# Last gate and final norm with half of the tokens on the partitions

## The chip, the cores and the metric

The kernel runs on one core of one Trainium2 chip. The metric is the device time of one execution in microseconds (us), as the median of several runs. Before the change it is 1174.45 us (median of 3 runs, 1174.26 to 1174.66).

## The reference

A decoder trunk of two layers over 512 tokens of 1024 features, in float32. Layer 0 is a gMLP mixer, layer 1 a sliding-window attention; after each mixer come a gated MLP (`conv_ffn`) and a gated per-layer embedding, and a final norm closes it. The change touches the last two steps for layer 1:

```python
def rmsnorm(x, g):
    xf = x.astype(jnp.float32)
    y = xf * lax.rsqrt(jnp.mean(xf * xf, axis=-1, keepdims=True) + EPS)
    return (y * g.astype(jnp.float32)).astype(x.dtype)

def per_layer_embed(h, p_i, g_norm, w_in, w_gate, b_gate):
    gate = jax.nn.sigmoid(rmsnorm(h, g_norm) @ w_gate + b_gate)
    return (p_i @ w_in) * gate

    h = h + conv_ffn(rmsnorm(h, norm_ffn[i]), f_w_up[i], f_conv_w[i], f_conv_b[i], f_w_down[i])
    h = h + per_layer_embed(h, p[i], norm_ple[i], ple_w_in[i], ple_w_gate[i], ple_b_gate[i])
return rmsnorm(h, norm_final)
```

In the kernel `p_i @ w_in` is called pin, `rmsnorm(h, g_norm) @ w_gate` gate.

## The kernel before, in words

**Layout.** The residual h lies feature-major: eight tiles `h[m]` of 128 features (on the partitions) by 512 tokens. A dense product is computed for one row block of 128 output features at a time: the weights are the stationary operand, the tokens the moving one.

**Precision.** Each float32 operand is split in two float32r halves, hi and lo. A product is three passes on TensorE (PE): hi x hi, lo x hi, hi x lo (`mm3`, lines 168 to 170; `mm3t`, lines 179 to 181, has the tokens as the stationary operand and so gives tokens on the partitions).

**Weight stream.** A list of pieces (`plan`, `plan_cols`, `plan_ffn`) is written ahead in the order of use. `load` (L124) brings a piece from DRAM with one DMA on SP's queue into one of three raw buffers (r0 to r2); `pump` splits it, hi on ScalarE (ACT, L141), lo on VectorE (DVE, L142), into a ring of `WBUFS` buffers (wh, wl) or, for the last two gate pieces, into tiles of their own (own_ah, own_al), which take the places of activations of the FFN that are no longer read. `chunk` hands the split pieces to the products. A load waits until its raw buffer's last split is done.

**Order of work.** PE's instructions stand in the order in which the program writes them, as do those of each other engine except where a scheduler moves an instruction ahead of others by priority. `ffn(1)` computes the up products in three parts; before the last part's down products stands `ple_in(1)` (pin: 48 matmuls of 512 columns, copied out of PSUM by ACT, L360). Then `dense_add` gives d0 to d7 (21 matmuls each), added to h by DVE (L301). As each h[m] is done, `Norm.take` scales and splits it into np1h and np1l (L210 on ACT, L211 on DVE), ACT squares it (L239) and POOL adds the squares up (L244).

**The tail (lines 704 to 799).** The gate is computed in two halves of the tokens, 256 moving columns each, in blocks of two row blocks (`gate(hf, c)`): 24 matmuls for a row block, k from 0 to 7 with three passes each. After gate(0, 0) `npl.begin` takes the mean square (`np1ms`, L255: four small products, then np1m on DVE and the inverse root np1rt on POOL, L268 and L270); after gate(0, 1) `npl.rstd` brings it onto the free dimension: np1dh and np1dl on DVE (L280, L281: a diagonal of the roots), np1sp on PE (L284, ones x diagonal), np1rstd on ACT (L262). `gated` is for each row block: z = gate x rstd (DVE, L725), sigmoid with the bias on its partitions (ACT, L727), times pin (DVE, L728), added to h (DVE, L730), squared (ACT, L732), the squares summed up on POOL (L739). `final_root(0)` stands behind the second half's first gate block, `final(0)` (spread, then y = h x gain x root on DVE, L759, with output DMAs of 256 KB) behind its second. For the second half the residual is turned token-major at the end: `dgain` (L751, diagonal matrices of the final gain, made early on DVE), `turn_back` (L783: 16 plain float32 products h x dgain, six row blocks ahead of the last root and two behind it), `final_root(1)` (L746), and y = ht x root on ACT (L798) and DVE (L796), out by four DMAs of 256 KB on ACT's and SP's queues (L799).

**At the start**, POOL makes small constants (ident, far, qscale), then waits for wsT's DMA (L433) and later computes n0rt (L270), while SP's queue loads vec, h and the first pieces of w_v, and PE begins the v products.

Of the kernel before, what the change touches and what calls it, by code (L numbers as in the profile page):

```python
# [8 lines left out]
F32 = mybir.dt.float32  # L9
# [4 lines left out]
P = 128  # L14
# [7 lines left out]
SLOTS = 9  # L22
HEADS = 16
# [23 lines left out]
def tile_yoco(ctx: ExitStack, tc: tile.TileContext, t, out: bass.AP, out_b: bass.AP):  # L47
# [26 lines left out]

    def plan_cols(w, n_chunks, kk, cols=256, k0=0):
        for c in range(n_chunks):
            plan(w[c, :, k0 * cols : (k0 + kk) * cols], kk * cols, cols)

# [38 lines left out]
    def load(upto):  # L117
        while state["raw"] < min(upto, len(pieces)):
# [5 lines left out]
            nc.sync.dma_start(r[:, :m], a)  # L124
# [27 lines left out]
    def chunk(cols, kk, ahead=WBUFS):  # L152
        """The next units that make up kk row blocks of `cols` columns, a triple for each."""
# [8 lines left out]
    def mm3(ps, parts, xs, c0, n=P, first=True, last=True):  # L162
        """ps += W[:, c0:c0+n]^T x over the row blocks, as three float32r passes."""
# [8 lines left out]
    def mm3t(ps, xs, parts, c0, n, tok, first=True, last=True):  # L172
        """ps += x[tokens]^T W[:, c0:c0+n]: tokens on partitions."""
# [9 lines left out]
    # ---- activations in  # L183
# [24 lines left out]
    # ---- helpers on activations  # L208
# [16 lines left out]
    class Norm:  # L225
        """Takes the residual's row blocks as they come: gains and splits them, sums the squares."""
# [24 lines left out]
        def begin(self):  # L251
            """One over the root mean square, tokens on the partitions."""
# [6 lines left out]
        def rstd(self):  # L259
            """The same along the free dimension, for every partition."""  # L260
# [12 lines left out]
    def spread(r, n, name):  # L273
        """[P, n] with tokens on the partitions -> [P, n * P], the tokens along it, in PSUM."""
# [18 lines left out]
    def dense_add(xs, kk, norm):  # L293
        """h += W^T x for the next kk row blocks of weights, 256 columns a chunk."""
# [10 lines left out]
    def ffn(l, norm, nxt):  # L305
        """Gated MLP, the hidden units in parts; the first of the next part goes before a part's products down."""
# [42 lines left out]
    def ple_in(l):  # L349
# [12 lines left out]
        return pe  # L362

# [22 lines left out]
    # ---- layer 0: gMLP mixer  # L386
# [26 lines left out]
    # minus the distance to the key, far away where the window or causality forbids it  # L413
# [7 lines left out]
    # queries over eight times a head's slope: logit = slope * (q k - distance)  # L421
# [10 lines left out]
    # positions attend to earlier ones alone: wsT[s, h, t] for s <= t  # L432
# [49 lines left out]

    npl = Norm("np0", [(xp, "x", gain("norm_ple", 0))])
# [4 lines left out]
    # ---- layer 1: shared K/V and sliding-window attention  # L488
# [3 lines left out]
    # keys of a group, their halves twice on the partitions, for the stacked halves of the queries  # L492
# [51 lines left out]
    # products beside attention's steps: each step is followed by some that need no result of it  # L544
# [21 lines left out]
    def merge(m, k0, k1):  # L566
        """Row block m of the output projection, from the heads that are done."""
# [36 lines left out]
    def scores(i):  # L604
        """Logits of a group's four heads over a block, their maximum with the sink, the exponentials."""
# [28 lines left out]
    def weights(i):  # L634
        """The exponentials over their sums."""
# [11 lines left out]
    def turn(i):  # L647
        """Probabilities, keys on the partitions."""
# [59 lines left out]
    N = S // 2  # L708
    half = [slice(hf * N, (hf + 1) * N) for hf in range(2)]
    parts, acc, last_sq, root = [], {}, {}, {}  # L710

    def gate(hf, c):
        if hf == 0:
            parts.append(chunk(256, KD))
        pss = []
        for j in range(2):
            ps = psum(f"gate{hf}_{c}_{j}")[:, :N]
            mm3(ps, parts[c], [(a[:, half[hf]], b[:, half[hf]]) for a, b in xs], j * P)
            pss.append(ps)
        return pss  # L720

    def gated(hf, c, pss):
        for m, ps in zip((2 * c, 2 * c + 1), pss):
            z = tp.tile([P, N], F32, tag="hs", name=f"z{hf}_{m}")
            nc.vector.tensor_mul(z, ps, rstd[:, half[hf]])  # L725
            sg = tp.tile([P, N], F32, tag="sg", name=f"gs{hf}_{m}")
            nc.scalar.activation(sg, z, AF.Sigmoid, bias=v("ple_b_gate", KD + m))  # L727
            nc.vector.tensor_mul(sg, sg, pe[m][:, half[hf]])  # L728
            hm = h[m][:, half[hf]]
            nc.vector.tensor_add(hm, hm, sg)  # L730
            sq = tp.tile([P, N], F32, tag="sq", name=f"fsq{hf}_{m}")
            nc.scalar.activation(sq, hm, AF.Square)  # L732
            if m == KD - 1:
                last_sq[hf] = sq
            elif m == 0:
                acc[hf] = sq
            else:
                a = tp.tile([P, N], F32, tag="c0", name=f"facc{hf}_{m}")
                nc.gpsimd.tensor_add(a, acc[hf], sq)  # L739
                acc[hf] = a  # L740

    def final_root(hf):
        ps = psum(f"fms{hf}")
        for c in range(N // P):
            for i, a in enumerate((acc[hf], last_sq[hf])):
                nc.tensor.matmul(ps[:, c : c + 1], a[:, c * P : (c + 1) * P], mean, start=i == 0, stop=i == 1)  # L746
        root[hf] = inv_root(ps[:, : N // P], f"fin{hf}")

    dgain = mp.tile([P, KD, P], F32, tag="m5", name="dgain")
    for m in range(KD):  # L750
        nc.vector.tensor_scalar_mul(dgain[:, m, :], ident, v("norm_final", m))  # L751

    def final(hf):
        r = spread(root[hf], N // P, f"fin{hf}")
        for c in range(4):
            y = (mp if c == 3 else wp).tile([P, 2, N], F32, tag="m4" if c == 3 else f"r{c}", bufs=1, name=f"y{hf}_{c}")
            for j in range(2):
                m = 2 * c + j
                nc.vector.scalar_tensor_tensor(y[:, j, :], h[m][:, half[hf]], v("norm_final", m), r,  # L759
                                               op0=ALU.mult, op1=ALU.mult)  # L760
            (nc.sync if c % 2 else nc.scalar).dma_start(
                out[2 * c : 2 * c + 2].rearrange("k p s -> p k s"), y)

    held = gate(0, 0)
    npl.begin()
    pss = gate(0, 1)
# [99 lines left out]
```

## Time and profile before

| | |
|---|---|
| median of 3 runs | 1174.45 us |
| span of the profiled execution | 1173.3 us |
| median less span | 1.15 us |
| PE, DVE, ACT, POOL busy | 98%, 65%, 46%, 7% of the span |
| bytes moved | 110.2 MB, 94 GB/s on average |

The span runs from the first to the last event of the profiled execution; the runs' times lie around it by the 1.15 us above. Times in rows of the timeline are microseconds from the span's start: start, duration, engine, line, operation, output<-inputs, how many merged instructions, and in brackets how long the engine had been idle before and what ended that. An engine name with q is its queue's issuing of DMAs. PE's matmuls overlap: a matmul's duration is longer than the distance to the next one, so the pitch (start to start) is what a matmul costs in a row of them. A window row gives the stretch, then busy time and count of PE, PEld, DVE, ACT and POOL, the granted clock, the DMA engines' busy share and GB/s. The groups of instructions give busy time in all and the mean in ns. DMA rows give count, KB and median time from issue to landing.

### The profile page before, as it was taken

Reading aid. Unit: us, or ns where it says so; the run is one execution under the profiler, and the core shown is the slowest. Engines: PE = TensorE matmul, PEld = TensorE weight load, DVE = VectorE, ACT = ScalarE, POOL = GpSimd, SP = SyncE. Lnnn points to the kernel's source line nnn. Section 1 sums busy time; section 2 is a strip of 40 time slices with the busy share of each in tenths; the row PEclk is TensorE's granted clock in tenths of the full one; section 3 lists DMA queues with packets and bytes.
Section 4 is the critical chain, followed back from the end, with each engine's and each line's share of the span. In section 5 each row is a group of like instructions: output and inputs, shape, how many; then the busy total and the mean of one; then the engine's idle time right before and its main releaser. Section 6 shows DMA issues by size and latency. Waiting matters only on the chain.

```text
span 1173.3 us, 14202 instructions
## 1 busy us (share of the span) xinstructions
PE 1152.2 (98%) x5634; PEld 968.3 (83%) x5634; DVE 761.8 (65%) x1229; ACT 543.0 (46%) x919; POOL 80.7 (7%) x86
## 2 busy tenths in 40 slices
PE   7999999999999999999989999999999999999998
PEld 7988888888888888888778767888888888888897
DVE  6365467763676377447779997577635773675665
ACT  5633444431344244445559986444313442345532
POOL 1000210000000000031220001100000000000221
PEclk9999999999999999999989999999999999999999
DMA  8222323322222333232212113322322333223302
GB/s 324 79 108 72 108 72 108 108 74 106 108 72 90 110 104 115 101 111 72 72 37 73 36 37 108 108 97 84 108 107 73 99 99 108 90 94 105 108 1 73
DMA packets 19011, 110.20 MB, mean 94 GB/s; under 512 B 2176, under 2 KB 3584, under 8 KB 8704
## 3 DMA queue, kind: packets, MB, share of 16 engines
q1 hardware_dynamic: 18112, 108.24, 26.5%
q10 hardware_dynamic: 832, 1.05, 0.3%
q8 instruction: 44, 0.72, 0.2%
q14 instruction: 23, 0.19, 0.1%
HBM read 107.19 MB, written 2.10 MB: 93 GB/s over the span
## 4 chain that ended last, share of the span: by engine, by line
PE 90%; DVE 6%; ACT 2%; issue 1%; DMA 0%; SPq 0%; POOLq 0%; POOL 0%; DVEq 0%; ACTq 0%
PE up L168 14%; PE up L170 14%; PE up L169 14%; PE d L168 8%; PE d L170 8%; PE d L169 8%; PE gate L169 2%; PE gate L168 2%; PE gate L170 2%; PE v L179 1%; PE v L180 1%; PE v L181 1%; PE u L168 1%; PE u L170 1%; PE u L169 1%; PE o L168 1%
## 5 line engine op out<-in xcount | busy, mean ns | idle before, releaser
L141 ACT CAST wh<-wraw 128x1024 fp32r<-128x1024 f32 (+1 forms) x198 | 203.0, 1026 | 272.8 <-PE d L169 132.2
L142 DVE TENSOR_TENSOR wl<-wraw,wh 128x1024 fp32r<-128x1024 f32 (+1 forms) x198 | 238.6, 1205 | 134.9 <-ACT wh L141 134.6
L168 PE MATMUL up<-nf00h,wh 128*128 128x512 f32 x352 | 137.2, 390 | 0.0
L168 PE MATMUL up<-nf10h,wh 128*128 128x512 f32 x352 | 137.2, 390 | 0.0
L170 PE MATMUL up<-nf10h,wl 128*128 128x512 f32 x352 | 137.1, 390 | 0.0
L170 PE MATMUL up<-nf00h,wl 128*128 128x512 f32 x352 | 137.1, 389 | 0.0
L169 PE MATMUL up<-nf00l,wh 128*128 128x512 f32 x352 | 137.1, 389 | 0.0
L169 PE MATMUL d<-al,wh 128*128 128x512 f32 x352 | 137.1, 389 | 0.0
L168 PE MATMUL d<-ah,wh 128*128 128x512 f32 x352 | 137.1, 389 | 0.0
L169 PE MATMUL up<-nf10l,wh 128*128 128x512 f32 x352 | 137.1, 389 | 0.0
L170 PE MATMUL d<-ah,wl 128*128 128x512 f32 x352 | 137.1, 389 | 0.0
L325 ACT ACTIVATE c<-hs,vec 128x512 f32<-128x512 f32 x88 | 71.5, 814 | 71.9 <-DVE hs L321 71.1
L326 DVE SCALAR_TENSOR_TENSOR c<-hs,vec,c 128x511 f32<-128x511 f32 x88 | 65.8, 749 | 34.2 <-ACT c L325 34.2
L301 DVE TENSOR_TENSOR h<-h,d 128x512 f32<-128x512 f32 x56 | 38.4, 687 | 73.7 <-PE d L170 73.7
L214 ACT CAST ah<-a 128x512 fp32r<-128x512 f32 x44 | 27.3, 621 | 109.1 <-DVE a L331 109.0
L170 PEld LDWEIGHTS up<-nf10h,wl 128*128 128x128 f32 x352 | 66.1, 188 | 13.8
L170 PEld LDWEIGHTS up<-nf00h,wl 128*128 128x128 f32 x352 | 66.1, 188 | 13.8
L170 PEld LDWEIGHTS d<-ah,wl 128*128 128x128 f32 x352 | 66.1, 188 | 13.7
L169 PEld LDWEIGHTS d<-al,wh 128*128 128x128 f32 x352 | 66.1, 188 | 13.7
L168 PEld LDWEIGHTS up<-nf00h,wh 128*128 128x128 f32 x352 | 66.1, 188 | 13.7
L169 PEld LDWEIGHTS up<-nf10l,wh 128*128 128x128 f32 x352 | 66.1, 188 | 13.6
L168 PEld LDWEIGHTS d<-ah,wh 128*128 128x128 f32 x352 | 66.1, 188 | 13.6
(281 smaller groups left out, 2195.4 us busy)
## 6 DMA issues: line engine op xcount, KB each, us to landing
wraw<-in_w_up SPq DMA_DIRECT2D x44, 1024.0 KB, 4.8
wraw<-in_w_down SPq DMA_DIRECT2D x16, 896.0 KB, 4.6
wraw<-in_w_down SPq DMA_DIRECT2D x8, 1024.0 KB, 4.9
wraw<-in_w_gate SPq DMA_DIRECT2D x8, 1024.0 KB, 4.8
wraw<-in_w_u SPq DMA_DIRECT2D x4, 1024.0 KB, 6.3
wraw<-in_w_out SPq DMA_DIRECT2D x4, 1024.0 KB, 4.7
wraw<-in_w_q SPq DMA_DIRECT2D x4, 1024.0 KB, 4.7
wraw<-in_w_o SPq DMA_DIRECT2D x4, 1024.0 KB, 4.8
```

Of the source, the lines that this page charges most:

```text
L141: nc.scalar.copy(wh[:, :n], src)
L142: nc.vector.tensor_sub(wl[:, :n], src, wh[:, :n].bitcast(F32))
L168: nc.tensor.matmul(ps, wh[:, a:b], xh, start=st, stop=False)
L169: nc.tensor.matmul(ps, wh[:, a:b], xl, start=False, stop=False)
L170: nc.tensor.matmul(ps, wl[:, a:b], xh, start=False, stop=en)
L179: nc.tensor.matmul(ps, xh[:, s], wh[:, a:b], start=st, stop=False)
L180: nc.tensor.matmul(ps, xl[:, s], wh[:, a:b], start=False, stop=False)
L181: nc.tensor.matmul(ps, xh[:, s], wl[:, a:b], start=False, stop=en)
L214: nc.scalar.copy(hi, src)
L301: nc.vector.tensor_add(h[m], h[m], ps)
L325: nc.scalar.activation(c, hs, AF.Identity, bias=v("conv_b", l * 2 * NJ + col), scale=cw[2])
L326: nc.vector.scalar_tensor_tensor(c[:, 1:], hs[:, : S - 1], cw[1], c[:, 1:], op0=ALU.mult, op1=ALU.add)
```

## The change

The gate and the final norm are computed feature-major for the first 256 tokens alone. For the second 256 tokens they are computed token-major.

- Pin: `ple_in_both` gives pef (feature-major, first half: 8 row blocks x 6 matmuls of 256 columns) and pet (token-major, second half: 2 token blocks x 2 x 6 matmuls of 512 columns).
- Gate weights of layer 1: `plan_pair` puts two column chunks side by side, four row blocks deep, in one piece; `load` brings it with two DMAs of 512 KB.
- First half: four row blocks open together in PSUM, first with k 0 to 5 for all, then k 6 and 7; `npl.begin` after the first of the four is complete, `npl.rstd` after all four.
- Then the second half's residual is transposed (16 products with ident, copied out by ACT to hT), and row blocks 4 to 7 of the first half follow.
- Second half: token blocks in cuts of 512 and 512 columns, the last in 512, 384 and 128. `gated_t`: z = gate x rt + bias row (DVE), sigmoid (ACT), times pet, plus hT (DVE), square with accumulation (ACT), times the gain row (POOL, the last cut on DVE); `final_t`: sum, inverse root, y scaled on ACT and DVE, two DMAs of 256 KB.
- The bias and the gain as rows: two DMAs on POOL's queue bring 1024 numbers each from the transposed view of vec into DRAM (`lines`), and two DMAs on SP's queue later broadcast them over the partitions (brow, grow).
- `dgain` and `turn_back` are gone. The first half's y is one tile, with four DMAs.

In the changed program's own order the two line DMAs stand among POOL's first instructions (one ahead of the last affine select of far, one behind it), and the row broadcasts on SP's queue ahead of the gate's loads. All other instructions up to pin stand as before. Lines after 706 of the kernel before are replaced as a whole; the diff shows the new ones alone there.

```diff
 SLOTS = 9
+N = S // 2
 HEADS = 16
...
             plan(w[c, :, k0 * cols : (k0 + kk) * cols], kk * cols, cols)
+    def plan_pair(w, k0, k1, own=None):
+        a_ = w[:, :, k0 * 256 : k1 * 256].rearrange("c p (k n) -> p k c n", n=256)
+        plan(a_, (k1 - k0) * S, S, own)
     def plan_ffn(l):
...
     plan_ffn(1)
-    plan_cols(t["w_gate"][1], 2, KD)
     free = [j % SLOTS for j in range(NJ, NJ + 8)]
     for c in range(2):
-        plan(t["w_gate"][1, 2 + c], 2 * UNIT, 256,
-             own=[(ap, f"ah{q}", f"al{q}") for q in free[4 * c : 4 * c + 4]])
+        for k0 in (0, 4):
+            plan_pair(t["w_gate"][1, 2 * c : 2 * c + 2], k0, k0 + 4,
+                      [(ap, f"ah{q}", f"al{q}") for q in free[k0 : k0 + 4]] if c else None)
     units = [(i, q, lo, n) for i, p in enumerate(pieces) for q, (lo, n) in enumerate(p[2])]
...
             state["turn"] += 1
-            nc.sync.dma_start(r[:, :m], a)
+            if len(a.shape) == 4:
+                for c in range(2):
+                    nc.sync.dma_start(r[:, :m].rearrange("p (k c n) -> p k c n", c=2, n=256)[:, :, c], a[:, :, c])
+            else:
+                nc.sync.dma_start(r[:, :m], a)
             raws[j] = r
...
             if last:
-                pe = ple_in(l)
+                pe = ple_in_both() if l else ple_in(l)
             nact = [] if last else [up(j1)]
...
         return pe
+    def ple_in_both():
+        pw = chunk(S, 2)
+        px = [(a[:, o : o + S], b[:, o : o + S]) for a, b, o in pw]
+        first = [(a[:, :N], b[:, :N]) for a, b in px]
+        feat, tok = [], []
+        for c in range(2):
+            parts = chunk(256, 4)
+            pf = mp.tile([P, 4, N], F32, tag=f"m{c}", name=f"pef{c}")
+            for j in range(4):
+                ps = psum(f"pinf{c}_{j}")[:, :N]
+                mm3(ps, parts[j // 2 * 2 : j // 2 * 2 + 2], first, j % 2 * P)
+                nc.scalar.copy(pf[:, j, :], ps)
+                feat.append(pf[:, j, :])
+            wh, wl = (x.rearrange("p (q k n) -> p q k n", q=2, k=2) for x in parts[0][:2])
+            for i in range(2):
+                if c == 0:
+                    tok.append(mp.tile([P, D], F32, tag=f"m{2 + i}", name=f"pet{i}"))
+                ps = psum(f"pint{c}_{i}")
+                s = slice(N + i * P, N + (i + 1) * P)
+                for k, (xh, xl) in enumerate(px):
+                    nc.tensor.matmul(ps, xh[:, s], wh[:, :, k, :], start=k == 0, stop=False)
+                    nc.tensor.matmul(ps, xl[:, s], wh[:, :, k, :], start=False, stop=False)
+                    nc.tensor.matmul(ps, xh[:, s], wl[:, :, k, :], start=False, stop=k == 1)
+                nc.scalar.copy(tok[i][:, c * S : (c + 1) * S], ps)
+        return feat, tok
     def ple(l, norm, nxt, pe):
...
     dense_add(us, KD, nf)
+    dram = ctx.enter_context(tc.tile_pool(name="dram", bufs=1, space=bass.MemoryType.DRAM))
+    lines = []
+    for name, l in (("ple_b_gate", 1), ("norm_final", 0)):
+        c0 = VEC[name] + l * KD
+        line = dram.tile([KD, P], F32, name=f"line_{name}")
+        with nc.allow_non_contiguous_dma(reason="1024 numbers"):
+            nc.gpsimd.dma_start(line, t["vec"][:, c0 : c0 + KD].rearrange("p m -> m p"))
+        lines.append(line.rearrange("m p -> (m p)"))
     npl = Norm("np0", [(xp, "x", gain("norm_ple", 0))])
...
     npl = Norm("np1", [(xp, "x", gain("norm_ple", 1))])
-    pe = ffn(1, nf, npl)
...
+    pef, pet = ffn(1, nf, npl)
+    xs = npl.xs[0][0]
+    half = slice(0, N)
+    first = [(a[:, half], b[:, half]) for a, b in xs]
+    facc = {}
+    def gated(m, ps):
+        z = tp.tile([P, N], F32, tag="hs", name=f"z{m}")
+        nc.vector.tensor_mul(z, ps, rstd[:, half])
+        sg = tp.tile([P, N], F32, tag="sg", name=f"gs{m}")
+        nc.scalar.activation(sg, z, AF.Sigmoid, bias=v("ple_b_gate", KD + m))
+        nc.vector.tensor_mul(sg, sg, pef[m])
+        hm = h[m][:, half]
+        nc.vector.tensor_add(hm, hm, sg)
+        sq = tp.tile([P, N], F32, tag="sq", name=f"fsq{m}")
+        nc.scalar.activation(sq, hm, AF.Square)
+        if m == 0:
+            facc[0] = sq
+        else:
+            a = tp.tile([P, N], F32, tag="c0", name=f"facc{m}")
+            nc.gpsimd.tensor_add(a, facc[0], sq)
+            facc[0] = a
+    parts = chunk(S, KD)
+    pss = [psum(f"gate{m}")[:, :N] for m in range(4)]
+    for m in range(4):
+        mm3(pss[m], parts[:6], first[:6], m * P, last=False)
+    for m in range(4):
+        mm3(pss[m], parts[6:], first[6:], m * P, first=False)
+        if m == 0:
+            rt = npl.begin()
+    rstd = npl.rstd()
+    for m in range(4):
+        gated(m, pss[m])
+    hT = [[at.tile([P, S], F32, tag=f"a{x}{i}", name=f"hT{i}_{x}") for x in "hl"] for i in range(2)]
+    for i in range(2):
+        for q in range(2):
+            ps = psum(f"ht{i}_{q}")
+            for m in range(4):
+                nc.tensor.transpose(ps[:, m * P : (m + 1) * P], h[4 * q + m][:, N + i * P : N + (i + 1) * P], ident)
+            nc.scalar.copy(hT[i][q], ps)
+    parts2 = chunk(S, KD, ahead=2 * WBUFS)
+    for m in range(4):
+        ps = psum(f"gate{4 + m}")[:, :N]
+        mm3(ps, parts2, first, m * P)
+        gated(4 + m, ps)
+    brow, grow = (mp.tile([P, D], F32, tag=tag, name=f"row_{tag}") for tag in ("m4", "m5"))
+    for r, line in zip((brow, grow), lines):
+        nc.sync.dma_start(r, line.partition_broadcast(P))
+    ssq = const.tile([P, 2, 4], F32, name="ssq")
+    total = const.tile([P, 2], F32, name="total")
+    rfin = const.tile([P, 2], F32, name="rfin")
+    yt = [wp.tile([P, D], F32, tag=f"r{1 + i}", bufs=1, name=f"yt{i}") for i in range(2)]
+    cuts = [[(0, 512), (512, 512)], [(0, 512), (512, 384), (896, 128)]]
+    def gate_t(i, n):
+        c0, w = cuts[i][n]
+        ps = psum(f"gt{i}_{n}")[:, :w]
+        mm3t(ps, xs, parts2 if c0 >= S else parts, c0 % S, w, 2 + i)
+        return ps
+    def gated_t(i, n, ps):
+        c0, w = cuts[i][n]
+        end = i == 1 and n == len(cuts[i]) - 1
+        z = tp.tile([P, w], F32, tag="hs", name=f"zt{i}_{n}")
+        nc.vector.scalar_tensor_tensor(z, ps, rt[:, 2 + i : 3 + i], brow[:, c0 : c0 + w], op0=ALU.mult, op1=ALU.add)
+        sg = tp.tile([P, w], F32, tag="sg", name=f"st{i}_{n}")
+        nc.scalar.activation(sg, z, AF.Sigmoid)
+        nc.vector.tensor_mul(sg, sg, pet[i][:, c0 : c0 + w])
+        hm = hT[i][c0 // S][:, c0 % S : c0 % S + w]
+        nc.vector.tensor_add(hm, hm, sg)
+        sq = tp.tile([P, w], F32, tag="sq", name=f"sqt{i}_{n}")
+        nc.scalar.activation(sq, hm, AF.Square, accum_out=ssq[:, i, n : n + 1])
+        if not end:
+            nc.gpsimd.tensor_mul(yt[i][:, c0 : c0 + w], hm, grow[:, c0 : c0 + w])
+        if end:
+            nc.vector.tensor_mul(yt[i][:, c0 : c0 + w], hm, grow[:, c0 : c0 + w])
+    def final_t(i):
+        n = len(cuts[i])
+        nc.vector.tensor_reduce(total[:, i : i + 1], ssq[:, i, :n], axis=mybir.AxisListType.X, op=ALU.add)
+        r = inv_root(total[:, i : i + 1], f"fin{1 + i}", 1.0 / D)
+        for q in range(2):
+            y = yt[i][:, q * S : (q + 1) * S]
+            if q:
+                nc.vector.tensor_scalar_mul(y, y, r)
+            else:
+                nc.scalar.activation(y, y, AF.Copy, scale=r)
+            (nc.sync if q else nc.scalar).dma_start(out_b[i, :, q * S : (q + 1) * S], y)
+    def final_root():
+        ps = psum("fms")
+        for c in range(N // P):
+            nc.tensor.matmul(ps[:, c : c + 1], facc[0][:, c * P : (c + 1) * P], mean, start=True, stop=True)
+        return inv_root(ps[:, : N // P], "fin0")
+    def final(root):
+        r = spread(root, N // P, "fin0")
+        y = wp.tile([P, KD, N], F32, tag="r0", bufs=1, name="y")
+        for m in range(KD):
+            nc.vector.scalar_tensor_tensor(y[:, m, :], h[m][:, half], v("norm_final", m), r,
+                                           op0=ALU.mult, op1=ALU.mult)
+            if m % 2:
+                (nc.sync if m % 4 == 1 else nc.scalar).dma_start(
+                    out[m - 1 : m + 1].rearrange("k p s -> p k s"), y[:, m - 1 : m + 1, :])
+    gated_t(0, 0, gate_t(0, 0))
+    root = final_root()
+    gated_t(0, 1, gate_t(0, 1))
+    final(root)
+    final_t(0)
+    for n in range(3):
+        gated_t(1, n, gate_t(1, n))
+    final_t(1)
```

More of the change, by code (lines that the diff above doesn't have):

```diff
@@ L704, in tile_yoco @@
     npl = Norm("np1", [(xp, "x", gain("norm_ple", 1))])
-    pe = ffn(1, nf, npl)
+    pef, pet = ffn(1, nf, npl)
     xs = npl.xs[0][0]
[L708 to L720, printed above, removed]
@@ L742, in final_root @@
-    def final_root(hf):
-        ps = psum(f"fms{hf}")
-        for c in range(N // P):
[L745 to L762, printed above, removed]
@@ L764, in tile_yoco @@
-    held = gate(0, 0)
-    npl.begin()
-    pss = gate(0, 1)
-    rstd = npl.rstd()
-    gated(0, 0, held)
-    gated(0, 1, pss)
-    for c in (2, 3):
-        gated(0, c, gate(0, c))
-    for c in range(4):
-        gated(1, c, gate(1, c))
-        if c == 0:
-            final_root(0)
-        if c == 1:
-            final(0)
-    turned = [[psum(f"ht{c}_{q}") for q in range(2)] for c in range(N // P)]
-    def turn_back(m):
-        for c, ps in enumerate(turned):
-            nc.tensor.matmul(ps[m // 4][:, m % 4 * P : (m % 4 + 1) * P],
-                             h[m][:, N + c * P : N + (c + 1) * P], dgain[:, m, :], start=True, stop=True)
@@ L786, in tile_yoco @@
-    for m in range(KD - 2):
-        turn_back(m)
-    final_root(1)
-    for m in (KD - 2, KD - 1):
-        turn_back(m)
-    for q in range(2):
-        for c, ps in enumerate(turned):
-            y = tp.tile([P, S], F32, tag=f"c{c}", name=f"y{c}_{q}")
-            r = root[1][:, c : c + 1]
-            if c:
-                nc.vector.tensor_scalar_mul(y, ps[q], r)
-            else:
-                nc.scalar.activation(y, ps[q], AF.Copy, scale=r)
-            (nc.sync if c else nc.scalar).dma_start(out_b[c, :, q * S : (q + 1) * S], y)
+    half = slice(0, N)
```

18 lines of the change are left out of this document (removed).

## The prediction

> **What bounds the kernel now.** I read the page first: the busy shares and the chain that ended last.
>
> ```profile
> span 1173.3 us, 14202 instructions
> ...
> PE 1152.2 (98%) x5634; PEld 968.3 (83%) x5634; DVE 761.8 (65%) x1229; ACT 543.0 (46%) x919; POOL 80.7 (7%) x86
> ...
> q10 hardware_dynamic: 832, 1.05, 0.3%
> ...
> PE 90%; DVE 6%; ACT 2%; issue 1%; DMA 0%; SPq 0%; POOLq 0%; POOL 0%; DVEq 0%; ACTq 0%
> ```
>
> TensorE is the bound: what lengthens its row of matmuls lengthens the kernel, and what is left over is the start, a few stalls and the end. The span is 1173.3 and the median 1174.45, so about 1.15 us lie around the span; I work on the span and add them. Before the last FFN's down products (d) the instruction order is the old one, except for two DMAs early on POOL. So I need the timeline from the d products on, and the start.
>
> ```profile
> 1074.65 0.39 PE L168 MATMUL d<-ah,wh 128*128 128x512 f32 x1
> ...
> 1112.73 0.28 PE L168 MATMUL gate<-np10h,wh 128*128 128x256 f32 x1
> ...
> 1162.25 0.28 PE L169 MATMUL gate<-np10l,own_ah 128*128 128x256 f32 x1
> ...
> 1162.73 0.28 PE L170 MATMUL gate<-np10h,own_al 128*128 128x256 f32 x1
> ```
>
> Pitches: the d products are 8 blocks of 21 matmuls, so (1112.73 - 1074.65) / 168 = 0.2267 us at 512 columns. The last two rows are four matmuls apart: 0.12 us at 256 columns. The gate takes 1112.73 to 1162.85 (one pitch after its last start), 50.12 us.
>
> **The change part by part.** First the gate's stall.
>
> ```profile
> 1117.81 0.39 PE L169 MATMUL gate<-np10l,wh 128*128 128x256 f32 x1 [1.33 <-DVE np10l L211]
> ...
> 1115.99 1.77 DVE L211 SCALAR_TENSOR_TENSOR np10l<-h,vec,np10h 128x512 fp32r<-128x512 f32 x1
> ...
> 1115.76 1.45 POOL L244 TENSOR_TENSOR np1acc<-np1acc,np1sq 128x512 f32<-128x512 f32 x1 [3.71 <-ACT np1sq L239]
> ```
>
> The third pass of block 0 waits for the low half of the last row block, whose split lasted 1.77 us beside a POOL addition. PE stood 1.33 us. After it the pitch was slow for some matmuls, so I take the loss from the sum: 50.12 less 384 x 0.12 = 46.08, less the small products (np1ms 0.8 and np1sp 0.5 by the rows below, the first half's root and spread some 1.0) leaves about 1.7. In the changed order 72 matmuls (k 0 to 5 of four blocks, 8.6 us) lie ahead of k 6 and 7, where 18 lay before: the split ends 5 us ahead of its need. **Gate0 stall: -1.7** (-1.3 if only the idle counts).
>
> Moved: np1ms now comes after block 0's k 6 and 7, and only 18 matmuls (2.2 us) follow before np1sp, where two whole blocks (48, 5.8 us) covered the chain through the root.
>
> ```profile
> 1120.07 0.95 PE L255 MATMUL np1ms<-mean,np1acc 128*128 128x1 f32 x8
> ...
> 1121.30 1.02 POOL L270 TENSOR_TENSOR np1rt<-np1m,minus_half 128x4 f32<-128x4 f32 x1 [4.10 <-DVE np1m L268]
> 1122.36 0.48 DVE L280 TENSOR_SCALAR np1dh<-ident,np1rt 128x128 fp32r<-128x128 f32 x2 [1.13 <-POOL np1rt L270]
> ...
> 1123.67 0.61 DVE L281 SCALAR_TENSOR_TENSOR np1dl<-ident,np1rt,np1dh 128x128 fp32r<-128x128 f32 x2
> ...
> 1126.72 0.40 PE L284 MATMUL np1sp<-np1dh,ones 128*128 128x512 f32 x1
> ...
> L746 PE MATMUL fms<-mean,facc 128*128 128x1 f32 x8 | 1.3, 230 | 0.0
> ```
>
> From np1ms' end (1121.02) to the last np1dl (1124.28) is 3.26 us, cover 2.2: PE stands 1.1 us, or 0.9 if the first of np1sp's two products (0.23, over all np1dh) is done before the last np1dl. At the other stall 1.33 idle cost 1.7, so a slow restart adds some 0.3. Queued behind np1sp on PE are the transposes and gates 4 to 7, all of which slip with it; DVE's z waits for rstd anyway. **np1sp stall: +1.2** (0.5 to 1.6).
>
> Added: 16 transposes of the second half's residual, ahead of gate 4. A row of the attention's transposes and the removed turn_back give the price:
>
> ```profile
> 642.55 0.38 PE L654 MATMUL tr<-ident,pr 128*128 128x128 f32 x2
> ...
> 1162.85 2.84 PE L783 MATMUL ht<-dgain,h 128*128 128x128 f32 x24
> ```
>
> The first says 0.11 each (0.38 less one's 0.27), the second 2.84 / 24 = 0.118 for a record, where a plain f32 product takes two. **Transposes: 16 x 0.11 = +1.8** (3.8 if they too take two records). turn_back goes, but its 24 records filled PE while it waited for z; only the last 8 come out of the end (below).
>
> Second half: 8 blocks x 24 x 0.12 = 23.04 become three token cuts of 512 columns and cuts of 384 and 128, 24 matmuls each: 72 x 0.2267 = 16.32; 384 columns are not in the trace, between 0.12 and 0.2267, I take 0.173 on the line through both: 4.15; 128 columns at 0.11 (the rows of the transposes are the nearest): 2.64. Sum 23.11, **+0.1** (-1.2 to +1.4 by the 384 bounds). The first half's 192 matmuls stay. The first half's root took eight records between the gates (half of the last row above and of its twin on the last squares, 0.1 us apart as np1ms' are) and takes four: **fms -0.4**. The pin products were 48 x 0.2267 = 10.88 and are 48 x 0.12 + 24 x 0.2267 = 11.20: **+0.3**. So the last gate product ends -1.7 + 1.2 + 1.8 + 0.1 - 0.4 + 0.3 = **1.3 later**.
>
> At nothing: dgain's eight DVE products go (they ran beside pin, where PE is the bound). Two row broadcasts of 512 KB come onto SP's queue ahead of the gate's loads once the pin products have freed their tiles, and each gate load becomes two of 512 KB with 1 KB rows.
>
> ```profile
> 1076.59 29.84 SPq L124 DMA_DIRECT2D wraw<-in_w_gate  x4
> ...
> wraw<-in_w_gate SPq DMA_DIRECT2D x8, 1024.0 KB, 4.8
> ```
>
> Four loads are issued over 29.8 us, one per 9.9, and land in 4.8: the queue is idle half of the time, and the 38 us of d products hide 1 MB more. Without that cover, see the rivals.
>
> **The end.** From the last gate slot to the first output DMA and on:
>
> ```profile
> 1163.05 0.42 DVE L725 TENSOR_TENSOR z<-gate,np1rstd 128x256 f32<-128x256 f32 x1 [0.99 <-PE gate L170]
> 1163.51 0.51 ACT L727 ACTIVATE gs<-z,vec 128x256 f32<-128x256 f32 x1 [0.94 <-DVE z L725]
> ...
> 1164.05 0.43 DVE L728 TENSOR_TENSOR gs<-gs,pe 128x256 f32<-128x256 f32 x1 [0.57 <-ACT gs L727]
> 1164.52 0.42 DVE L730 TENSOR_TENSOR h<-h,gs 128x256 f32<-128x256 f32 x1
> 1165.03 0.42 ACT L732 ACTIVATE fsq<-h 128x256 f32<-128x256 f32 x1 [1.01 <-DVE h L730]
> ...
> 1165.53 0.28 PE L746 MATMUL fms<-mean,facc 128*128 128x1 f32 x2
> ...
> 1166.52 0.16 DVE L268 TENSOR_SCALAR fin1m<-fms 128x2 f32<-128x2 f32 x1 [1.58 <-PE fms L746]
> 1166.76 0.71 POOL L270 TENSOR_TENSOR fin1rt<-fin1m,minus_half 128x2 f32<-128x2 f32 x1 [3.32 <-DVE fin1m L268]
> 1167.50 1.26 ACT L798 ACTIVATE y<-ht,fin1rt 128x512 f32<-128x512 f32 x2 [2.05 <-PE ht L783]
> ...
> 1168.22 0.93 ACTq L799 DMA_DIRECT2D out<-y  x2
> ```
>
> Before: 1162.85 to 1168.22, 5.37 us. After, on a last cut of 128 columns: drain 0.2; z 0.34, sigmoid 0.40, product 0.28, sum 0.28, square 0.32 with its accumulated sum read out 0.2 (estimates, below the 256-column rows by the step that the 128-column diagonals above, 0.31 to 0.35, stand at; the read-out isn't in these rows, 0 to 0.4); reduce 0.17 and m 0.16 on DVE (the fin1m row); root 0.71; one y of 512 columns 0.63 (half of 1.26); nine hand-overs of 0.05 (1163.47 to 1163.51 and the like). Sum 4.14: **-1.2** (-0.6 if the 128-column steps cost what the 256-column ones do).
>
> Behind the issue: four DMAs of 256 KB, 1168.22 to 1173.3, 5.08 us, move 1.05 MB:
>
> ```profile
> 1170.00:1171.00 1.00, 0.00 (x0) 0.00 (x0) 0.00 (x0) 0.00 (x0) 0.00 (x0) 0.90 1.01 385
> ...
> out<-y ACTq DMA_DIRECT2D x4, 256.0 KB, 2.4
> ```
>
> After, only the last 128 tokens' two DMAs are left. Half the bytes at 385 GB/s is 1.36 us less, and the second issue on each queue (half of the 0.93) falls away partly under it. **Output -1.5** (to 3.6; the floor is the 2.4 us landing plus the close, so -2.2 at most, -1.0 if small writes don't speed up).
>
> **The start.** The two early POOL DMAs fetch 1024 numbers each from the transposed view: 2048 elements of 4 bytes, DRAM to DRAM, among the memsets near 3 to 4 us. Nothing in the trace does that.
>
> ```profile
> 10.00:15.00 5.00, 5.00 (x43) 5.00 (x43) 4.45 (x7) 5.00 (x9) 0.00 (x0) 1.00 1.06 408
> 15.00:20.00 5.00, 5.00 (x44) 5.00 (x43) 4.90 (x7) 4.57 (x8) 0.00 (x0) 1.00 1.01 404
> ...
> 13.25 1.93 ACT L210 ACTIVATE n00h<-h,vec 128x512 fp32r<-128x512 f32 x3
> ...
> 5.17 2.69 SPq L195 DMA_DIRECT2D h<-in_xT  x4
> ...
> 4.10 0.40 POOL L419 TENSOR_SCALAR_AFFINE_SELECT far<-far 128x256 f32<-128x256 f32 x1
> 20.18 1.16 POOL L433 TENSOR_SCALAR_AFFINE_SELECT wsT<-wsT 128x1024 f32<-128x1024 f32 x1 [15.68 <-DMA wsT<-in_wsT]
> 32.77 2.08 POOL L270 TENSOR_TENSOR n0rt<-n0m,minus_half 128x4 f32<-128x4 f32 x1 [11.43 <-DVE n0m L268]
> ```
>
> The 16 DMA engines are full from 10 to 20 us (shares 1.06 and 1.01) while PE already runs on what they just brought: the last x blocks are issued up to 7.9 and split from 13.25 on, so a delay of the loads beyond some 0.5 to 1 us reaches PE. POOL itself idles 15.7 and 11.4 us there, so making the descriptors is hidden unless it lasts beyond wsT and n0rt. The price of a packet: q10's 832 packets take 0.3% of 16 engines' 1173.3 us, 0.068 us each, at 1.26 KB. By that row 2048 of them fill all 16 engines for 8.7 us; by their bytes nothing. Only those ahead of the last x block by about 14 us can hurt, at most half, and a 4-byte packet should cost a third or so of a 1.26 KB one: 1024 x 0.023 / 16 = 1.5, less 0.5 of slack, **+1.0** (0 to 8).
>
> [...]
>
> **Sum.** 1.3 - 1.2 - 1.5 + 1.0 = -0.4: 1172.9 in the span, **1174.0** with what lies around it.
>
> **The rivals.**
>
> *The line DMAs hold up the start (slower).* For it: the full DMA engines at 10 to 20 us, PE's dependence on them, and a price by the row of up to 8.7 us. Against: POOL idle, little data. From 3.75 us of delay on (-1.4 + 3.75 = +2.35) the kernel is slower; at the middle of 0 and 8, 4 us, it gives 1177. [...]
>
> *The gains come and the costs don't.* The spread runs through its first products (stall 0.5), the line DMAs cost nothing (0), the output shrinks by 2.2: 0.6 - 1.2 - 2.2 + 0 = -2.8, **1171.6**. For it: the 2.4 us landing of the earlier output DMAs; against: the end's DMAs take longer than that in this trace.
>
> *Gate loads late (slower).* Eight DMAs of 1 KB rows for four of 8 KB rows; a piece is due each 9.9 us and took 4.8 to land, so they must be twice slower before PE waits; half of the output DMAs above have 1 KB rows, and their median landing is 2.4 us for 256 KB. At three times slower (14.4 us) the last piece is 4.5 us late, less the 1.2 of the np1sp stall that it takes over: 1177.3.
>
> *The change doesn't shorten the end.* The read-out of the sums, POOL's products beside DVE (the 1.77 us row shows what they do to each other) and the transposes at two records: end -0.3, transposes 3.8, the rest as summed: 1.3 + 2.0 - 0.3 - 1.5 + 1.0 = +2.5, 1176.95.
>
> **How the numbers follow.** A difference under about 0.2% (2.35 us: 1172.1 to 1176.8) can't be told from no change. Forecast near the sum, 0.56, its own range 1172.1 to 1176.8; larger gain 0.22; line DMAs slower 0.12; late gate loads 0.03; end not shorter 0.07. Faster 0.22, same 0.56, slower 0.22. For 8 in 10 the range goes from 1171.3 to 1177.4.
>
> **What would show it.** Right: the first gate product 0 to 3 us later than 1112.73 + 0.3 by the start's delay and nothing else; no idle PE at gate0's np10l; about 1 us of idle at np1sp; 16 transposes in 1.8 us; 4.1 us from last gate product to first output DMA; one pair of output DMAs at the end. Wrong: idle PE between 6.8 and 30 us of several us, waits of the gate for wh or own_ah, a sigmoid or square on 128 columns as long as on 256, or POOL's root late behind its products.

## The result and the profile after

The changed kernel takes 1193.23 us (median of 4 runs, 1191.12 to 1194.78) where the kernel before, run beside it, takes 1174.56 (1174.26 to 1175.16). The ratio is 1.0157, 95% interval 1.0145 to 1.0169: slower by 18.7 us. The profiled execution has a span of 1190.4 us, 17.1 more than before. Lines of the changed kernel are those of its own file, ten higher in the helpers (L178 to L180 for `mm3`, L189 to L191 for `mm3t`).

The page of the changed kernel:

```profile
span 1190.4 us, 14058 instructions
...
PE 1152.6 (97%) x5558; PEld 965.1 (81%) x5558; DVE 758.1 (64%) x1216; ACT 544.8 (46%) x926; POOL 85.1 (7%) x88
...
q0 software_dynamic: 96, 0.02, 0.4%
...
PE 89%; DVE 5%; ACT 2%; DMA 2%; issue 1%; POOL 0%; SPq 0%; POOLq 0%; ACTq 0%
```

PE's busy time is the same within 0.4 us. What came is idle time. The chain has a new DMA share of 2%, and a queue q0 (POOL's; q1 is SP's, q10 ACT's) with hardly any bytes is there. The timeline of the start shows both:

```profile
4.00 1.28 POOL L527 DMA_DIRECT2D line_ple_b_gate<-in_vec  x1
...
5.69 1.08 POOL L527 DMA_DIRECT2D line_norm_final<-in_vec  x1
...
21.80 1.04 ACT L151 CAST wh<-wraw 128x1024 fp32r<-128x1024 f32 x1 [8.69 <-DMA wraw<-in_w_v]
30.36 0.72 ACT L220 ACTIVATE n00h<-h,vec 128x512 fp32r<-128x512 f32 x1 [7.51 <-DMA h<-in_xT]
...
14.72 0.28 PE L191 MATMUL v<-wl,n00h 128*128 128x256 f32 x1
31.13 0.58 PE L189 MATMUL v<-wh,n00h 128*128 128x256 f32 x1 [16.13 <-ACT n00h L220]
...
32.51 0.41 PE L189 MATMUL v<-wh,n00h 128*128 128x256 f32 x1
32.72 0.41 PE L190 MATMUL v<-wh,n00l 128*128 128x256 f32 x1
```

POOL issues the two line DMAs in 1.28 and 1.08 us. PE then runs until 14.84 and stands 16.1 us: it waits for ACT's split, ACT for the loads of w_v and x. After the stop the pitch is 0.21 us until 35.28, in place of 0.12, so the start loses more than the idle time. The windows give the DMA engines' share and GB/s (last two columns; the third from the end is the granted clock):

```profile
10.00:15.00 5.00, 5.00 (x35) 4.67 (x34) 1.83 (x3) 1.46 (x3) 0.00 (x0) 1.00 1.69 24
15.00:20.00 5.00, 0.00 (x1) 0.00 (x0) 0.00 (x0) 0.00 (x0) 0.00 (x0) 0.83 0.45 21
20.00:25.00 5.00, 0.00 (x0) 0.00 (x0) 1.23 (x1) 1.04 (x1) 0.00 (x0) 0.50 0.95 180
25.00:30.00 5.00, 0.00 (x0) 0.00 (x0) 0.00 (x0) 0.00 (x0) 0.00 (x0) 0.50 1.06 80
30.00:35.00 5.00, 3.67 (x15) 3.37 (x16) 3.43 (x5) 4.53 (x7) 0.00 (x0) 0.50 0.47 112
```

Where before 408 and 404 GB/s came (10 to 15 and 15 to 20 us), 24 and 21 come. The granted clock falls here to 0.50 while PE stands, and is still 0.50 after it starts again; from 30 to 35 us the 0.50 goes with the 0.21 us of pitch. PE's first products, from 7.77 to 11.18 us, have the pitch of 0.21 too, where the same view has the clock at 1.00 (5 to 15 us): there the two don't agree.

From here on, the tail. The kernel before starts its pin products here:

```profile
1063.77 0.39 PE L168 MATMUL pin<-own_m,wh 128*128 128x512 f32 x1
```

And the changed kernel, from pin to the last output:

```profile
1082.63 0.28 PE L178 MATMUL pinf<-own_m,wh 128*128 128x256 f32 x1
...
1093.87 0.39 PE L178 MATMUL d<-ah,wh 128*128 128x512 f32 x1
...
1131.95 0.28 PE L178 MATMUL gate<-np10h,wh 128*128 128x256 f32 x1
...
1144.23 0.28 PE L180 MATMUL gate<-np10h,wl 128*128 128x256 f32 x1
1145.04 0.49 PE L294 MATMUL np1sp<-np1dh,ones 128*128 128x512 f32 x1 [0.53 <-DVE np1dh L290]
1145.57 0.50 PE L294 MATMUL np1sp<-np1dl,ones 128*128 128x512 f32 x1
1145.90 1.91 PE L796 MATMUL ht<-ident,h 128*128 128x128 f32 x16
1147.57 0.36 PE L178 MATMUL gate<-np10h,own_ah 128*128 128x256 f32 x1
...
1176.28 0.33 PE L189 MATMUL gt<-own_ah,np10h 128*128 128x384 f32 x1
...
1180.47 0.22 PE L189 MATMUL gt<-own_ah,np10h 128*128 128x128 f32 x1
...
1182.98 0.28 PE L191 MATMUL gt<-own_al,np10h 128*128 128x128 f32 x1
...
1183.30 0.35 DVE L826 SCALAR_TENSOR_TENSOR zt<-gt,np1rt,row_m 128x128 f32<-128x128 f32 x1 [0.27 <-PE gt L191]
...
1184.95 0.19 ACT L833 ACTIVATION_READ_ACCUMULATOR sqt<-hT_l 128x1 f32 x1
...
1185.59 0.55 POOL L280 TENSOR_TENSOR fin2rt<-fin2m,minus_half 128x1 f32<-128x1 f32 x1 [1.49 <-DVE fin2m L278]
...
1186.93 0.35 ACTq L849 DMA_DIRECT2D out<-yt  x1
```

With these rows the 17.1 us come apart, each stretch as after less before:

| stretch | before | after | difference | forecast |
|---|---|---|---|---|
| start to first pin product | 1063.77 | 1082.63 | +18.86 | +1.0 |
| pin (to the first d product) | 10.88 | 11.24 | +0.36 | +0.3 |
| first to last gate product | 50.12 | 51.14 | +1.02 | +1.0 |
| last gate slot to ACT's last output group | 5.37 | 3.84 | -1.53 | -1.2 |
| from there to the span's end | 5.08 | 3.47 | -1.61 | -1.5 |

(1183.09, a pitch of 0.11 after 1182.98, ends the gate.) The tail moved by -1.76 where -1.4 was forecast. The whole loss is in the start.

### The profile page after: what moved, and what is told of

Same layout as the page of the kernel before. It is cut to its first block, busy times and chain, and to the rows that moved or that the text cites. A ratio compares the mean times of both kernels' runs of the same rounds, so it can differ in the third digit from the quotient of the medians.

```text
span 1190.4 us, 14058 instructions
## 1 busy us (share of the span) xinstructions
PE 1152.6 (97%) x5558; PEld 965.1 (81%) x5558; DVE 758.1 (64%) x1216; ACT 544.8 (46%) x926; POOL 85.1 (7%) x88
## 4 chain that ended last, share of the span: by engine, by line
PE 89%; DVE 5%; ACT 2%; DMA 2%; issue 1%; POOL 0%; SPq 0%; POOLq 0%; ACTq 0%
PE up L178 13%; PE up L179 13%; PE up L180 13%; PE d L179 8%; PE d L180 8%; PE d L178 8%; DMA h<-in_xT 2%; PE gate L178 2%; PE gate L180 2%; PE gate L179 2%; PE u L180 1%; PE u L179 1%; PE u L178 1%; PE v L190 1%; PE v L191 1%; PE v L189 1%
## 5 line engine op out<-in xcount | busy, mean ns | idle before, releaser
L178 PE MATMUL up<-nf00h,wh 128*128 128x512 f32 x352 | 137.1, 389 | 0.0
L178 PE MATMUL up<-nf10h,wh 128*128 128x512 f32 x352 | 137.1, 389 | 0.0
L180 PE MATMUL up<-nf00h,wl 128*128 128x512 f32 x352 | 137.0, 389 | 0.0
L180 PE MATMUL up<-nf10h,wl 128*128 128x512 f32 x352 | 137.0, 389 | 0.0
L178 PE MATMUL d<-ah,wh 128*128 128x512 f32 x352 | 136.9, 389 | 0.0
L180 PE MATMUL d<-ah,wl 128*128 128x512 f32 x352 | 136.9, 389 | 0.0
L178 PEld LDWEIGHTS up<-nf00h,wh 128*128 128x128 f32 x352 | 66.1, 188 | 13.8
L180 PEld LDWEIGHTS up<-nf00h,wl 128*128 128x128 f32 x352 | 66.1, 188 | 13.8
L178 PEld LDWEIGHTS d<-ah,wh 128*128 128x128 f32 x352 | 66.1, 188 | 13.7
L180 PEld LDWEIGHTS up<-nf10h,wl 128*128 128x128 f32 x352 | 66.1, 188 | 13.7
L180 PEld LDWEIGHTS d<-ah,wl 128*128 128x128 f32 x352 | 66.1, 188 | 13.7
```

The lines of the kernel that those rows point to most:

```text
L178: nc.tensor.matmul(ps, wh[:, a:b], xh, start=st, stop=False)
L180: nc.tensor.matmul(ps, wl[:, a:b], xh, start=False, stop=en)
```

## The experiments

**Theory:** the two line DMAs hold up the loads, and nothing else of the change costs. **Rivals:** something else at the start does; POOL's software queue does, whatever it moves; a price per element. In the table, the ratio to the kernel before run beside it, and the first pin product's start, which shows the start's delay alone (one profile each; runs spread by up to some us where the start is disturbed). e2, e3, e6 and e8 have two runs each, and e9's profile is of its slowest run, 1177.55 us, where its other seven took 1173.86 to 1175.58. A cost in us is the difference to e1's ratio times 1174.56:

| version | median us | ratio, 95% interval | first pin product |
|---|---|---|---|
| before | 1174.56 | | 1063.77 |
| the change | 1193.23 | 1.0157 (1.0145 to 1.0169) | 1082.63 |
| e1_no_lines | 1173.35 | 0.9987 (0.9977 to 0.9996) | 1063.69 |
| e2_lines_alone | 1195.62 | 1.0176 (1.0156 to 1.0197) | 1082.84 |
| e3_lines_on_act | 1197.82 | 1.0195 (1.0175 to 1.0216) | 1089.09 |
| e4_lines_contiguous | 1173.74 | 0.9988 (0.9978 to 0.9998) | 1063.38 |
| e5_gather_to_sbuf | 1178.25 | 1.0028 (1.0017 to 1.0039) | 1068.29 |
| e6_one_line | 1182.10 | 1.0063 (1.0045 to 1.0082) | 1070.56 |
| e8_scatter_from_sbuf | 1182.19 | 1.0064 (1.0046 to 1.0083) | 1072.35 |
| e9_spread_writes | 1174.80 | 1.0000 (0.9990 to 1.0011) | 1068.05 |
| e12_spread_64_bytes | 1178.90 | 1.0037 (1.0025 to 1.0050) | 1068.36 |
| e10_lines_at_60us | 1173.23 | 0.9987 (0.9977 to 0.9997) | 1063.56 |
| e7_lines_by_tensore | 1173.94 | 0.9995 (0.9986 to 1.0004) | 1064.45 |
| e11_early_lines_early_root | 1172.77 | 0.9984 (0.9975 to 0.9993) | 1063.64 |

**Whose is it?** Without the line DMAs (e1, whose rows are then broadcast from x), and with them alone in the kernel before (e2). The diff shows e1's edit; e2 adds the same lines to the other kernel:

```diff
...
-            nc.gpsimd.dma_start(line, t["vec"][:, c0 : c0 + KD].rearrange("p m -> m p"))
...
+    lines = [t["xT"][0, 0:2].rearrange("p s -> (p s)"), t["xT"][0, 2:4].rearrange("p s -> (p s)")]
```

> The changed kernel without the two line DMAs; bias and gain rows are broadcast from 4 KB of the input x instead, so the values of bias and gain are wrong in the second half. Theory (the line DMAs block the loads at the start, and nothing else is lost): the start is as in the kernel before, first pin product at 1063.8 us, and the rest as in the changed kernel's trace, 1.4 later at the last gate product and 3.1 shorter behind it: about 1172.7 us. Rival (the loss comes from something else that the change does at the start, code or buffers): about 1191 as before.

> The kernel before with the two line DMAs alone, their result unused. Theory: the whole loss of the start is theirs, 18 to 19 us: about 1193. Rival (they hurt only with the rest of the change): about 1174.5.

Both as the theory has it: without them the start is the old one (1063.69) and the kernel is 1.5 us faster than before, with them alone it loses 19.1 us at the start. The rest of the change is worth 0.0013 of the time.

**Queue or elements?** e3 writes `nc.scalar.dma_start` for `nc.gpsimd.dma_start`; e4 keeps POOL's queue:

```diff
-            nc.gpsimd.dma_start(line, t["vec"][:, c0 : c0 + KD].rearrange("p m -> m p"))
+            nc.gpsimd.dma_start(line, t["xT"][l, 0:KD, 0:P])
```

> The changed kernel with the two line DMAs on ACT's queue in place of POOL's; they then stand at the head of that queue, near 1 to 2 us. If the price is that of 2048 elements of 4 bytes, whoever issues them: about 1190 again. If it is that of POOL's software queue: about 1172.7.

> The changed kernel with the line DMAs still on POOL's queue, but copying 8 runs of 512 bytes each out of x, in place of 1024 single numbers; bias and gain are wrong in the second half. If the price is that of the elements: about 1172.7. If it is that of the software queue or of a DRAM to DRAM copy as such: about 1190.

The queue is not it: contiguous lines on POOL's queue cost nothing that can be told, and elements on ACT's cost more (1197.82 us, where about 1190 was expected). There they stand ahead of the first loads, and every element is a packet of its own (2064 packets on ACT's queue below, for 2048 elements), where POOL's queue made 96 packets of them all; which of the two makes it worse isn't shown. POOL's issuing isn't what costs the time either: e3 doesn't use that queue, e4 uses it and loses nothing that can be told, and POOL's rows above took 1.28 and 1.08 us. The DMA queues of e3 from 0 to 40 us:

```profile
q1 hardware_dynamic: 2192, 4.68, 64.9%
q10 hardware_dynamic: 2064, 0.01, 15.7%
```

15.7% of 16 engines times 40 us is 100 us for 2064 packets, 0.049 us each on average, 6.3 us for an engine. That alone would not lose 25 us. The loads' own packets are held up: the changed kernel's queues from 4 to 30 us, and then from 10 to 15 us alone,

```profile
q1 hardware_dynamic: 1688, 3.47, 95.0%
q0 software_dynamic: 96, 0.02, 16.8%
...
line_ple_b_gate<-in_vec POOLq DMA_DIRECT2D x1, 4.0 KB, 17.8
line_norm_final<-in_vec POOLq DMA_DIRECT2D x1, 4.0 KB, 25.0
```

```profile
q1 hardware_dynamic: 56, 0.11, 114.7%
q0 software_dynamic: 27, 0.01, 54.7%
```

against the kernel before, from 4 to 30 us and from 10 to 15 us:

```profile
q1 hardware_dynamic: 2853, 9.22, 95.2%
```

```profile
q1 hardware_dynamic: 827, 2.04, 105.7%
```

From 4 to 30 us the share of the loads is the same, 95%, but for 3.47 MB in place of 9.22. From 10 to 15 us a packet of the loads took 1.057 x 80 / 827 = 0.102 us before (16 engines times 5 us are 80) and now takes 1.147 x 80 / 56 = 1.64 us on average, sixteen times as long. It is not that each is slow: in the packet records 16 of the 56 took over 1 us, the longest 9.0, and the median is 0.165. A packet counts whole in the window in which it starts, which is how a share passes 1; over 10 to 20 us the shares of 1.69 and 0.45 come to 1.07. The engines look full and move next to nothing.

**How many, and which side?** One line only (e6); reads from DRAM but writes into an SBUF tile of 8 rows (e5); reads from vec in SBUF but writes the same places (e8); the same reads, but the numbers written 512 bytes (e9) or 64 bytes (e12) apart:

```diff
 # e5
...
+            nc.gpsimd.dma_start(lsb, t["vec"][:, c0 : c0 + KD].rearrange("p m -> m p"))
+        nc.gpsimd.dma_start(line, lsb)
 # e8
...
+            nc.gpsimd.dma_start(line.rearrange("m p -> p m"), vec[:, c0 : c0 + KD])
 # e9 (e12: [D, 16])
...
+        line = dram.tile([D, P], F32, name=f"line_{name}")
...
+            nc.gpsimd.dma_start(line.rearrange("(m p) x -> m p x", m=KD)[:, :, 0],
+                                t["vec"][:, c0 : c0 + KD].rearrange("p m -> m p"))
```

> The changed kernel with one line DMA of 1024 elements in place of two; the gain row stands in for the bias too, so the bias is wrong in the second half. If the price goes with the number of elements, half of 18.9 us: about 1182 to 1184. If the first one alone blocks the queues: 1188 or more.

> The changed kernel, but each line is gathered as 1024 single numbers from DRAM into an SBUF tile of 8 rows, and goes on from there to DRAM in 8 runs of 512 bytes. If 4-byte writes to neighbouring places of DRAM are what is slow: about 1173 to 1176. If it is the number of elements (or the scattered 4-byte reads): 1188 to 1194.

> The changed kernel, but the line DMAs read vec's tile in SBUF (8 numbers side by side on 128 partitions) in place of vec in DRAM, and write the same 1024 single numbers into DRAM. If the 4-byte writes to DRAM are slow: 1188 or more. If the scattered 4-byte reads from DRAM are: about 1173 to 1176.

> The changed kernel with the two element DMAs where they were, but each number written 512 bytes from the next in DRAM in place of 4; the rows are broadcast from x, so bias and gain are wrong in the second half. If small writes to neighbouring places get in each other's way: the write part goes, about 1178 as with the gather to SBUF. If each element has its price wherever it goes: 1190 to 1195.

> As the version with numbers written 512 bytes apart, but 64 bytes apart (8 numbers in 512 bytes in place of 128; bias and gain wrong in the second half, as there). If only numbers that share 64 bytes of DRAM get in each other's way: about 1174.8 again. If those that share 512 bytes do: between the two, 1177 to 1185.

One line costs 0.0076 over e1 (1.0063 less 0.9987), 8.9 us; two cost 0.0170, 20.0 us, which is twice as much within e6's interval. e5 (4.8 us), e8 (9.0) and e9 fell outside both times that had been expected of each. e5 and e8 taken alone looked like a price for reads and one for writes. e9 speaks against that: with the same count, the same scattered reads and the same 4-byte writes it costs 1.5 us (0.0013) in place of 20.0, and as its interval overlaps e1's, even these 1.5 us aren't shown. What it takes away is that the writes lie side by side. e12 stands between, 5.9 us, clear of both by its interval. So with the same reads the time falls as the writes lie farther apart: 4, 64 and 512 bytes from one to the next give 20.0, 5.9 and 1.5 us. That the distance itself counts is one reading of this. Writes farther apart also cover more of DRAM (4, 64 and 512 KB for a line), and no run separates the two.

Distance isn't all, either. e8 writes the same numbers to the same places as the changed kernel and costs 9.0 us, not 20.0. Its edit changes two things at once: the reads come from SBUF, and the order `p m` takes the eight numbers of a partition in turn, which lie 512 bytes apart. By e9 scattered reads alone are worth far less than these 11 us; whether it is the order, or reads and writes together, isn't shown.

The landing of the line DMAs (17.8 and 25.0 us in the changed kernel) falls with the distance too; e12, then e9:

```profile
line_ple_b_gate<-in_vec POOLq DMA_DIRECT2D x1, 4.0 KB, 8.6
line_norm_final<-in_vec POOLq DMA_DIRECT2D x1, 4.0 KB, 10.9
```

```profile
line_ple_b_gate<-in_vec POOLq DMA_DIRECT2D x1, 4.0 KB, 8.0
line_norm_final<-in_vec POOLq DMA_DIRECT2D x1, 4.0 KB, 9.3
```

Why writes that lie side by side cost more isn't shown, and why writes into SBUF (e5), where the numbers of a row lie side by side too, cost 4.8 us isn't either. That stays open.

**Does it hurt everywhere?** e10 holds the same element DMAs back by writing to the lines first from a tile that waits for the gMLP's root:

```diff
...
+    lz = const.tile([KD, P], F32, name="lz")
+    nc.vector.tensor_scalar_mul(lz, ident[:KD], rv[:KD, 0:1])
...
+        nc.gpsimd.dma_start(line, lz)
...
+            nc.gpsimd.dma_start(line, t["vec"][:, c0 : c0 + KD].rearrange("p m -> m p"))
```

> The changed kernel with the same two element DMAs, held back until the gMLP's norm root is there (about 60 us), where the DMA engines are 23% to 29% busy and POOL is idle for 60 us. If what hurt is that they meet loads on which PE waits: the cost is hidden, about 1173 to 1174. If they hold up the loads wherever they are put: two times 12 us against a load due each 11 to 12 us with two or three pieces ahead, PE stands some us, 1178 or more.

It is hidden whole: the ratio is e1's, 0.9987. Its windows and its DMAs from 58 to 100 us:

```profile
65.00:70.00 5.00, 5.00 (x32) 4.45 (x31) 3.28 (x4) 2.59 (x4) 2.19 (x2) 1.00 0.29 3
70.00:75.00 5.00, 5.00 (x23) 4.14 (x23) 3.67 (x6) 1.22 (x2) 0.00 (x0) 1.00 0.66 8
75.00:80.00 5.00, 5.00 (x23) 4.14 (x23) 1.92 (x2) 1.69 (x2) 0.00 (x0) 1.00 0.63 53
```

```profile
wraw<-in_w_out SPq DMA_DIRECT2D x4, 1024.0 KB, 7.0
...
line_ple_b_gate<-in_vec POOLq DMA_DIRECT2D x1, 4.0 KB, 14.4
line_norm_final<-in_vec POOLq DMA_DIRECT2D x1, 4.0 KB, 20.0
```

The DMAs are as slow as ever (14.4 and 20.0 us), the loads of w_out beside them take 7.0 us (4.7 in the kernel before), yet PE is busy 5.00 of 5.00 us: the pieces that are already there last until the next ones come.

**A version that beats both.** e7 makes the lines on the chip, where the lines stood in the program; e11 does so before PE's first product, and takes the root earlier:

```diff
...
+        nc.tensor.transpose(lps[:KD, i * P : (i + 1) * P], vec[:, c0 : c0 + KD], ident)
+    nc.vector.tensor_copy(lsb, lps[:KD, : 2 * P])
...
+        nc.gpsimd.dma_start(line, lsb[:, i * P : (i + 1) * P])
 # e11 besides
...
+    rt = npl.begin()
     for m in range(4):
         mm3(pss[m], parts[6:], first[6:], m * P, first=False)
-        if m == 0:
-            rt = npl.begin()
```

> The changed kernel, but the two lines are made on the chip: two transposes of vec's columns on TensorE, one copy on DVE, and two DMAs of 8 runs of 512 bytes each on POOL's queue. Theory (only the elements hurt): like the kernel without line DMAs, 0.998 to 0.9995 of the kernel before, about 1173.2 us, with correct values. Rival (fetching rows early is what costs, however it is done): over 1180.

> Two mends of the changed kernel: the lines by TensorE (two transposes of vec's columns before PE's first product, when it has nothing to do) in place of the element DMAs; and the mean square np1ms taken between the two rounds of the first half's products (24 small products ahead of np1sp in place of 18). With the start free and 0.5 us of the wait at np1sp gone: 1.4 + 0.5 = 1.9 us under the kernel before, ratio 0.9984, about 1172.6 us. If the DMAs of the lines still delay the first loads: 1174 or more; if np1ms then waits for np1acc: no gain over the version without that move, about 1173.2.

e7's interval holds 1, so no gain is shown for it. e11 is at 0.9984 (0.9975 to 0.9993), 1.9 us under the kernel before, as expected; its PE rows around the start and np1sp:

```profile
3.47 0.59 PE L431 MATMUL lps<-ident,vec 128*8 128x128 f32 x2 [3.47 <-DMA vec<-in_vec]
6.53 0.58 PE L189 MATMUL v<-wh,n00h 128*128 128x256 f32 x1 [2.47 <-ACT n00h L220]
```

```profile
1121.60 0.95 PE L265 MATMUL np1ms<-mean,np1acc 128*128 128x1 f32 x8
1125.36 0.47 PE L294 MATMUL np1sp<-np1dh,ones 128*128 128x512 f32 x1
1125.86 0.50 PE L294 MATMUL np1sp<-np1dl,ones 128*128 128x512 f32 x1
1126.19 1.91 PE L800 MATMUL ht<-ident,h 128*128 128x128 f32 x16
```

The two transposes sit in the time in which PE waits for its first split anyway, and no wait stands in brackets at np1sp any more. Its lead over e1 (0.9987) lies within the intervals of the two.

## Why the prediction was wrong

The step that failed is the last term of its sum, "The start": +1.0 (0 to 8) forecast, +18.86 measured. The path was seen and named (full DMA engines, elements of 4 bytes among them, PE waiting for the last x blocks), and given as a rival with a chance of 0.12, at 1177. What the prediction had wrong is how the elements hurt: it counted the engine time of their own packets, and what cost the time is that the loads' packets beside them nearly stopped. Three choices made the term so small.

- *The price of a packet.* It was taken from the nearest row by queue (0.068 us at 1.26 KB), scaled down to a third for the few bytes, for 2048 packets. No run shows that third; it was the author's estimate. In the changed kernel the queue shows 96 packets in their place, 0.168 x 416 / 96 = 0.73 us each; where every element is a packet (e3), one took 0.049 us on average. So neither the count nor the scaling was borne out.
- *The upper bound.* 2048 packets by the price of the row were held to be the most that the elements could take, 8.7 us. The recorded time of the elements stays below it (16.8% of 16 engines' 26 us are 70 us, 4.4 for an engine). What the bound leaves out is that the packets of the other queue became slow beside them, 1.64 us on average for 0.102. Here the time of a queue's own packets was no bound on what they did to another queue's.
- *"At most half" of the elements ahead of the last x block.* The loads nearly stop soon after the elements' first packet, which the packet records have at 8.8 us: 24 GB/s come from 10 to 15 us, and the fifth of the eight x blocks is split at 30.36, where it was split at 12.11 before.

The other steps held. Gate0's stall: PE's list of waits has none for np10l; the -1.7 isn't measured by itself. np1sp: its first product starts 0.69 us after its slot (1144.35) and the second 0.30 after its own, 1.0 where 1.2 was forecast. Transposes: 1.67 (1145.90 to 1147.57) for 1.8. The cut of 384 columns took 4.19 (1176.28 to 1180.47) for 4.15, the one of 128 took 2.62 for 2.64. Pin +0.36 for +0.3. The end -1.53 for -1.2: the 128-column steps are short (z 0.35, the read-out 0.19, as estimated) and the root took 0.55 for 0.71. The output -1.61 for -1.5. Of the rivals, late gate loads didn't happen (no wait of the gate for weights in PE's list), and neither did an end that stays as long.

## What to carry to other kernels

Before two small DMAs are counted as nothing, count their elements and look where they are written: 8 KB in 4-byte pieces written side by side cost 20.0 us here, in contiguous rows (e4, 0.9988 beside e1's 0.9987) nothing that could be told. Look where a scheduler puts a DMA that waits for nothing: it went to the very start, where PE then stood 16.1 us for the loads; the same DMA at 60 us was free (e10, 0.9987). And the time of one queue's packets, 4.4 us for an engine here, was no bound for its harm to the others, 18.86 us.

## What the runs showed of the hardware

Small writes to neighbouring places held up the loads beside them here: at the start of this kernel 2048 writes of 4 bytes cost 20.0, 5.9 and 1.5 us at 4, 64 and 512 bytes from one to the next (the last within the noise of nothing). In the changed kernel the load packets took 1.64 us on average from 10 to 15 us in place of 0.102, with a median of 0.165, and from 10 to 20 us the engines' recorded share was 1.07 on average at 24 and 21 GB/s: the high share was no sign of bytes being moved. Into SBUF (e5) such elements cost 4.8 us. Why they do this isn't shown.
